# Stores from GpSimd's queue, and the recurrence stage's instruction order planned with other durations and with transfer queues that work in order

## The chip, the cores and the metric

The kernel runs on one core of one Trainium2 chip. The metric is the time of one execution on the device, in microseconds (us), as the median of several runs. In what follows PE is TensorE, DVE is VectorE, ACT is ScalarE, POOL is GpSimd and SP is SyncE. The engines work in parallel. Each takes its own instructions in the order in which the program holds them, and waits on semaphores for what the others make. SP computes nothing here: it issues DMA transfers.

## The reference, cut to what matters

Two requests, x_prompt and x_sample (512 tokens of 1024 features each, float32), pass through the same two layers. Layer 0 is a bidirectional RWKV-7 time mixing with 16 heads of 64, layer 1 a two-dimensional neighbourhood attention.

```python
def _wkv7_scan(r, decay, k, v, a, b, reverse):
    def step(s, inp):
        r_t, w_t, k_t, v_t, a_t, b_t = inp
        sa = jnp.einsum('bhvk,bhk->bhv', s, a_t)
        s = s * w_t[:, :, None, :] + sa[..., None] * b_t[:, :, None, :] + v_t[..., None] * k_t[:, :, None, :]
        return s, jnp.einsum('bhvk,bhk->bhv', s, r_t)
...
    # _rwkv7_branch: r, k, v are products of shifted inputs, z of the input
    kk = kk / jnp.maximum(jnp.sqrt(jnp.sum(kk * kk, axis=-1, keepdims=True)), 1e-12)
    for d in range(2):
        w_log = -jax.nn.softplus(-(w0[d] + jnp.tanh(xw @ w1[d]) @ w2[d]).astype(f32)) - 0.5
        decay = heads(jnp.exp(-jnp.exp(w_log)))
        a = heads(jax.nn.sigmoid((a0[d] + (xa @ a1[d]) @ a2[d]).astype(f32)))
        k_d = k * (1.0 + (a - 1.0) * k_a_h)
        ys.append(_wkv7_scan(r, decay, k_d, v, -kk, kk * a, reverse=(d == 1)))
...
def _trunk(x, ...):
    for i in range(DEPTH):
        xn = _rms_norm(x, pre_norm_g[i])
        h = _rwkv7_branch(xn, ...) if i % 2 == 0 else _natten_branch(xn, ...)
        x = x + _rms_norm(h, post_norm_g[i])
```

## The kernel before

Activations lie with features on the 128 partitions and the 512 tokens along the free dimension, so a request is 8 tiles of 128x512. A large product of a 128-column block of a weight with a request is built from 8 *triples*: weight and input are each split into a high and a low fp32r part, and a triple is three 128x512 matmuls (lines 404 to 406 outside the recurrence stage, 738 to 740 inside it). The split of a weight costs one ACT cast and one DVE subtraction per half (lines 699 and 701).

The program has three stages. The **prelude** normalises both requests and computes z and k of the first. The **recurrence stage** (`scan_phase`) computes both requests' time mixing. The **rest** does the attention layer.

In the recurrence stage each request has 4 head groups, so there are 8 groups in a row. The scan runs in chunks of 64 tokens, 8 *steps* per group, 64 steps in all, each needing the state S of the step before. Beside this chain of steps run these threads:

- `flow` (line 699 and on): the large products that the stage still owes, 76 columns of 8 triples, 608 triples in all, always in the same order: r and v of request 0, k, r and v of request 1, the output product of request 0, z of request 1, and then the first products of the attention layer. They fill PE while the chain of steps waits.
- `prep`: for each group, the factors `ab` of both scan directions, stored to DRAM as `dab` (1024 KB each store), and the Gram blocks (line 886).
- `inverse`: for each group, the inverse of a triangular matrix by 30 elimination rounds on DVE (lines 928, 929) and small matmuls (957, 959); its result MT is also cleared in part by POOL (line 946).
- `fetch`, `fetch_x`: loads of `cab`, `V` and `X` of each step from DRAM (`dab`, `dvt`).
- `near`, `outer`: the parts of a step that need no state (lines 1005, 1009 and 1030, 1038, 1045).
- `step`: lines 1075 and 1081 make Z, ACT copies it (1087), 1097 applies MT, ACT copies X (1108), 1113 and 1118 make the new state and the output, DVE scales the state (1123).
- `finish`: normalises the output of a group, multiplies by z and stores y.

Some gates tie the chain to the flow: a group's steps begin when its columns of v exist (`fetch` in `scan_phase`). The fifth group is the first of request 1 and needs 34 columns, 272 triples, of the flow. The seventh group waits until the fifth is finished, which needs z of request 1: 50 columns, 400 triples.

The order in which PE, DVE and ACT get the instructions of this stage is decided when the program is built. `weave` asks which thread could go on now, and the class `Clock` is its planner: it keeps a model time for every engine, adds a duration to it for every instruction recorded (`one`, `matmul`), and tells when a tile will be ready (`at`) or a buffer free (`room`). The lowest rank among the threads that are ready comes next. For SP the model only adds 380 ns per transfer; it does not hold SP back when a transfer must wait for its data. The order on SP and POOL, and everything outside the stage, is set by the framework's scheduler.

All transfers, loads and stores alike, are issued by SP (`load` and `save`, lines 306 and 309, and two direct calls at 1389 and 1455). POOL does memsets only: 32 of them clear the pad column of the tile `e1` (line 828), one for each direction of each head pair.

## Time and profile before

| | us |
|---|---|
| median of 3 runs (1751.27 to 1755.62) | 1752.39 |
| profiled execution: span from first to last instruction | 1748.0 |
| PE busy in it | 1604.4 (92%) |
| DVE busy | 1213.3 (69%) |
| ACT busy | 973.6 (56%) |
| POOL busy | 24.1 (1%) |

The profiled execution has no time of its own beside its span, so the span is compared with the median: 4.4 us lie between them. The 16 DMA engines moved 336.26 MB. An engine's busy time is the union of its instructions' intervals. A matmul's interval holds its whole way through the array, and the next one starts before it ends; so two 64x64 matmuls of 222 ns each may follow each other much closer than 222 ns. Waits are put down to the event that came last. An `SPq` row is SP's queue: the time in which SP issues a transfer or waits to do so; it is not part of any busy time.

### The profile page before, as it was taken

To read this page: it belongs to the slowest core of one execution; us is meant where nothing else is said; L and a number is where in the kernel's file an instruction comes from. 1 tells how busy PE (TensorE), PEld (TensorE's weight loads), DVE (VectorE), ACT (ScalarE), POOL (GpSimd) and SP (SyncE) were. 2 spreads that over 40 slices of the span, in tenths; PEclk is the share of its full clock that TensorE was granted. 3 is DMA by queue.
4 is the path that set the end of the run, shared out by engine and by line. 5 is a ranking of instruction groups with operands and counts; after the bars stand their busy time and mean duration, and the time that the engine had idled before them with its cause. 6 is when DMAs were issued, how large, how long until landed. Compare 5 with 4: busy or idle time off the path is not lost.

```text
span 1748.0 us, 46203 instructions
## 1 busy us (share of the span) xinstructions
PE 1604.4 (92%) x18816; PEld 1228.1 (70%) x18816; DVE 1213.3 (69%) x2645; ACT 973.6 (56%) x1964; POOL 24.1 (1%) x94
## 2 busy tenths in 40 slices
PE   7999788998999996898998988999999999999998
PEld 6766665765766674666766676787777788777776
DVE  8976588788888569796888857423556686555564
ACT  5444665666664565666666444333556664555462
POOL 0000000000000000000000000000000000000000
PEclk9989988999999997999999989999999999999999
DMA  5436677685666657777556766554555347545552
GB/s 201 163 115 211 219 266 221 204 269 190 213 198 209 198 172 254 221 213 251 186 187 216 247 200 201 186 204 139 175 184 166 103 132 262 174 155 158 162 175 97
DMA packets 240821, 336.26 MB, mean 192 GB/s; under 512 B 53697, under 2 KB 119361, under 8 KB 240609
## 3 DMA queue, kind: packets, MB, share of 16 engines
q1 hardware_dynamic: 240608, 333.31, 58.7%
q8 instruction: 148, 2.42, 0.6%
q14 instruction: 65, 0.52, 0.1%
HBM read 227.71 MB, written 105.51 MB: 191 GB/s over the span
## 4 chain that ended last, share of the span: by engine, by line
PE 61%; DVE 17%; DMA 8%; ACT 7%; issue 5%; SPq 1%; DVEq 0%; ACTq 0%
PE pg L404 6%; PE pg L405 6%; PE pg L406 6%; PE pm L738 5%; PE pm L739 5%; PE pm L740 5%; PE pm L1331 3%; DVE etmp L928 2%; PE po L1359 2%; PE pt L1346 2%; DVE N L929 2%; PE pf L1030 2%; DVE ab L851 2%; DMA cab<-dab 2%; PE zy L404 1%
## 5 line engine op out<-in xcount | busy, mean ns | idle before, releaser
L738 PE MATMUL pm<-act,whi 128*128 128x512 f32 x608 | 268.6, 442 | 17.9 <-ACT whi L699 8.0
L739 PE MATMUL pm<-act,whi 128*128 128x512 f32 x608 | 246.8, 406 | 19.0 <-DVE act L723 18.7
L740 PE MATMUL pm<-act,wlo 128*128 128x512 f32 x608 | 245.1, 403 | 2.3 <-DVE wlo L701 2.3
L404 PE MATMUL pg<-act,whi 128*128 128x512 f32 x448 | 181.6, 407 | 0.4 <-ACT whi L353 0.4
L405 PE MATMUL pg<-act,whi 128*128 128x512 f32 x448 | 178.4, 398 | 0.0
L406 PE MATMUL pg<-act,wlo 128*128 128x512 f32 x448 | 177.9, 397 | 0.0
L354 DVE TENSOR_TENSOR wlo<-raw,whi 128x512 fp32r<-128x512 f32 x156 | 107.0, 688 | 93.3 <-ACT whi L353 80.5
L353 ACT CAST whi<-raw 128x512 fp32r<-128x512 f32 x156 | 96.2, 618 | 131.6 <-PE pg L405 62.5
L701 DVE TENSOR_TENSOR wlo<-raw,whi 128x512 fp32r<-128x512 f32 x152 | 103.2, 686 | 84.4 <-ACT whi L699 83.1
L738 PEld LDWEIGHTS pm<-act,whi 128*128 128x128 f32 x608 | 117.7, 194 | 54.9 <-ACT whi L699 9.3
L739 PEld LDWEIGHTS pm<-act,whi 128*128 128x128 f32 x608 | 118.3, 195 | 44.9 <-DVE act L723 24.3
L740 PEld LDWEIGHTS pm<-act,wlo 128*128 128x128 f32 x608 | 118.3, 195 | 30.2 <-DVE wlo L701 4.4
L699 ACT CAST whi<-raw 128x512 fp32r<-128x512 f32 x152 | 93.0, 618 | 73.0 <-PE pm L739 55.8
L404 PEld LDWEIGHTS pg<-act,whi 128*128 128x128 f32 x448 | 84.3, 188 | 24.5 <-issue 9.1
L405 PEld LDWEIGHTS pg<-act,whi 128*128 128x128 f32 x448 | 84.3, 188 | 18.4 <-issue 3.5
L406 PEld LDWEIGHTS pg<-act,wlo 128*128 128x128 f32 x448 | 84.2, 188 | 18.2 <-issue 2.2
L929 DVE TENSOR_TENSOR N<-etmp,N 128x30 f32<-128x30 f32 (+14 forms) x240 | 79.8, 332 | 8.2
L1342 ACT ACTIVATE sb<-sb,mx 128x256 f32<-128x256 f32 x128 | 64.1, 502 | 37.6 <-DVE mx L1341 37.1
L928 DVE TENSOR_TENSOR etmp<-N 128x30 f32<-128x30 f32 (+14 forms) x240 | 78.7, 328 | 4.4
L1339 DVE CUSTOM_DVE_ANT_0 sb<-pm,bias 128x256 f32<-128x256 f32 x128 | 50.3, 421 | 45.1 <-PE pm L1331 34.2
L1045 ACT COPY Tm<-pf 128x512 f32<-128x512 f32 x56 | 32.8, 586 | 86.5 <-DVE R L1038 86.5
L1030 PE MATMUL pf<-cab 64*64 64x128 f32 (+1 forms) x2048 | 71.8, 279 | 9.3 <-DMA cab<-dab 6.8
(369 smaller groups left out, 3372.1 us busy)
## 6 DMA issues: line engine op xcount, KB each, us to landing
dab<-ab SPq DMA_DIRECT2D x32, 1024.0 KB, 5.8
cab<-dab SPq DMA_DIRECT2D x64, 512.0 KB, 4.5
raw<-in_w_in_dram SPq DMA_DIRECT2D x128, 256.0 KB, 3.0
bias<-in_rpb_dram SPq DMA_DIRECT2D x32, 384.0 KB, 4.3
raw<-in_w_z_dram SPq DMA_DIRECT2D x32, 256.0 KB, 4.4
dz<-tmp SPq DMA_DIRECT2D x32, 256.0 KB, 2.3
raw<-in_w_k_dram SPq DMA_DIRECT2D x32, 256.0 KB, 3.2
dk<-tmp SPq DMA_DIRECT2D x32, 256.0 KB, 2.2
```

The lines of the kernel that those rows point to most:

```text
L353: self.nc.scalar.copy(hi, src)
L354: (eng or self.nc.vector).tensor_tensor(lo, src, hi.bitcast(F32), op=ALU.subtract)
L404: nc.tensor.matmul(ps, hi, x[k][0], start=(k == 0), stop=False)
L405: nc.tensor.matmul(ps, hi, x[k][1], start=False, stop=False)
L406: nc.tensor.matmul(ps, lo, x[k][0], start=False, stop=(k == KT - 1))
L701: nc.vector.tensor_tensor(lo, raw.pop(h), hi.bitcast(F32), op=ALU.subtract)
L738: nc.tensor.matmul(ps, hi[:, at], xh, start=(k == 0), stop=False)
L739: nc.tensor.matmul(ps, hi[:, at], xl, start=False, stop=False)
L740: nc.tensor.matmul(ps, lo[:, at], xh, start=False, stop=(k == KT - 1))
L928: vt.tensor_tensor(tv, N[:, q + 1:, q:q + 1].broadcast_to([P, n, q]), N[:, q:q + 1, :q].broadcast_to([P, n, q]), op=ALU.mult)
L929: vt.tensor_tensor(N[:, q + 1:, :q], tv, N[:, q + 1:, :q], op=ALU.add)
L1030: end = nc.tensor.matmul(f[half(a), h, 0, d, g] if st.last else f[half(a), h, :, d, g], ab[half(h), d, g, 2 * e[d] + a], rt if st.last els ...
```

## The change

Three things are changed.

**Stores.** A new method `store` issues a transfer from POOL's queue. `save`, the stores of `dss`, `drn`, `dvt` and `dab`, and both stores of the outputs go through it. Of the 1290 transfers 358 move from SP to POOL. Loads stay on SP. A load of what a store wrote still waits for that store.

**The planner.** `Clock` gets other durations and latencies, a cost for ACT's function tables, and a queue `Q` for POOL's transfers (1000 ns each). SP and `Q` now work in order in the model: a transfer that must wait for its data or its buffer holds the ones behind it. Three gates on loads ask whether the buffer is free before the thread is chosen. The threads, their ranks and their gates are the same otherwise. The computation is the same.

**The pad of e1.** One tile `e1` with a pad column at either end takes the place of one per direction; it is cleared once, ahead of the stage.

```diff
-    LAT = dict(P=200.0, A=45.0, D=45.0, G=90.0, S=0.0)
+    LAT = dict(P=200.0, A=125.0, D=118.0, G=150.0, S=0.0, Q=0.0)
...
+    def free(self, tag, pool, bufs):
+        x = self.room((tag, id(pool)), bufs)
+        return x if x < 1e11 else 0.0
...
+            if e == "G" and "DMA" in type(i).__name__.upper():
+                e = "Q"
...
-                    if f != e or e == "S":
+                    if f != e or (e in "SQ" and table is self.made) or (table is self.made and e != "P"):
                         t = max(t, at)
...
-        elif e == "S":
-            self.t[e] = issued = max(issued, self.t["P"]) + 380.0
+        elif e in "SQ":
+            issued = self.t[e] = max(t, self.t["P"]) + (380.0 if e == "S" else 1000.0)
+            if e == "Q":
+                self.t["G"] = issued
...
-                c = 175.0 + 0.86 * n
...
+            if table != self.table:
+                c += 1283.0
+            return c + (50.0 if bank(ins[0]) else 90.0) + (2.0 if wide else 0.835) * n
...
     def save(self, kind, s, p, src):
         self.sp[kind, s, p] = d = self.dram(f"{kind}{s}{p}", src.shape)
-        self.nc.sync.dma_start(d, src)
+        self.store(d, src)
+
+    def store(self, dst, src):
+        self.nc.gpsimd.dma_start(dst, src)
...
-            e1 = b("e1", (P, NCH, L + 1))
-            pad = L * d
-            gps.memset(e1[:, :, pad:pad + 1], 1.0)
-            e1v, e0v = e1[:, :, 1 - d:L + 1 - d], e1[:, :, d:L + d]
+            e1 = self.e1
+            e1v, e0v = e1[:, :, 1:L + 1], e1[:, :, 2 * d:L + 2 * d]
...
-            self.load(sp["ab", s, pb][:, :, d, g, :].rearrange("c p a -> p c a"), ab.rearrange("p c a t -> p c (a t)"))
+            self.store(sp["ab", s, pb][:, :, d, g, :].rearrange("c p a -> p c a"), ab.rearrange("p c a t -> p c (a t)"))
...
-                        nc.sync.dma_start(self.a["y"][1][ms, j * T:j * T + T], hs[j, m])
+                        self.store(self.a["y"][1][ms, j * T:j * T + T], hs[j, m])
...
                 yield (
                     "S", lambda: did["states"] >= q - 1 and did["preps"] > st.n and ("v", st.s, 2 * st.pb + 1) in self.made,
-                    lambda c: c.at([self.sp["ab", st.s, st.pb].tensor.name]))
+                    lambda c: max(
+                        c.at([self.sp["ab", st.s, st.pb].tensor.name]), c.free("V", self.front, self.NX),
+                        max(c.used.get(self.cab[q % 2].tensor.name, {}).values(), default=0.0)))
```

The instructions of PE and DVE are the same in number and kind before and after. On ACT there are 6 more loads of a function table, 30 for 24. What moves is the order. Three places show how.

The first is PE between the last step of the second group and the first of the third. Before, from one L1097 (the application of MT) to the next, these are the first 12 rows of 19; `pm` with `act` and `whi` or `wlo` is a flow triple, the rest belongs to steps, `prep` and `inverse`:

```order
L1097 MATMUL us_6177<-Z_6148,MT_440_1697 64x64 x8
L1005 MATMUL zy_6118<-cab_441_1698 64x64 x8
L959 MATMUL pm_6198<-MT_439_1696,NA_5837 32x32 x32
L1118 MATMUL zy_6118<-X_5959,R_6015 64x64 x8
L625 MATMUL pm_6250<-tmp_6238,cc 2x512
L1081 MATMUL zy_6268<-V_5990,AK_6188 64x64 x8
L1030 MATMUL pf_6280<-cab_442_1699 64x2x64 x16
L807 MATMUL pm_6303<-h_127_637,w2h_5917 128x512
L808 MATMUL pm_6303<-h_127_637,w2l_5916 128x512
L959 MATMUL pm_6309<-MT_439_1696,NA_5837 32x32 x32
L807 MATMUL pm_6351<-h_138_673,w2h_5917 128x512
L808 MATMUL pm_6351<-h_138_673,w2l_5916 128x512
```

With the change the same place begins like this (lines are those of the changed kernel: 1122 is the old 1097, 1143 the old 1118, 765 to 767 the old 738 to 740):

```order
L1122 MATMUL us_5798<-Z_5780,MT_441_1700 64x64 x8
L765 MATMUL pm_5482<-act_4054,whi_4960 128x512
L766 MATMUL pm_5482<-act_4053,whi_4960 128x512
L767 MATMUL pm_5482<-act_4054,wlo_4961 128x512
L1143 MATMUL zy_5748<-X_5608,R_5699 64x64 x8
L765 MATMUL pm_5482<-act_4307,whi_4960 128x512
L766 MATMUL pm_5482<-act_4306,whi_4960 128x512
L767 MATMUL pm_5482<-act_4307,wlo_4961 128x512
L765 MATMUL pm_5858<-act_2518,whi_5166 128x512
L766 MATMUL pm_5858<-act_2517,whi_5166 128x512
L767 MATMUL pm_5858<-act_2518,wlo_5167 128x512
L765 MATMUL pm_5858<-act_3313,whi_5166 128x512
```

Before, 2 triples stand between these two steps; now 54 do. Over the stage, the triples that stand ahead of the first L1097 of the eight groups are 116, 159, 178, 210, 306, 334, 438 and 448 before, and 124, 159, 228, 255, 321, 397, 448 and 484 now. Ahead of the last L1097 of the fourth group stand 228 and now 275, of the sixth 354 and now 415; ahead of the last L1118 of all, 465 and now 508.

The second place is SP at the load of `k` for the second head pair of the sixth group. Before (`k`, `r`, `lora` are what `prep` loads, `raw` are weights for the flow; `dvt`, `dab`, `dks` and `dv` on the left are stores):

```order
L309 DMA dvt_1696_9187<-vs_9298 64x8x64 x2
L309 DMA dvt_1696_9187<-vs_9313 64x8x64 x2
L309 DMA dab_1661_9064<-ab_9273 128x8x256
L309 DMA raw_9337<-in_w_v_dram 128x512
L309 DMA k_9463<-dk_1080_5127 128x512
L309 DMA dvt_1696_9187<-vs_9403 64x8x64 x2
L309 DMA raw_9428<-in_w_v_dram 128x512
L309 DMA tmp_9471<-in_lora_dram 128x512
L306 DMA dks_1729_9401<-kp_1691_9173 128x512
L309 DMA r_9464<-dr_1553_8533 128x512
L306 DMA dv_1738_9438<-tmp_9436 128x512
L309 DMA dvt_1696_9187<-vs_9444 64x8x64 x2
```

With the change, SP at the same load (L336 is the new line of `load`):

```order
L336 DMA rb_9902<-drn_1266_6330 64x512 x2
L336 DMA bv_12051<-dv_1570_8438 128x512
L336 DMA raw_9633<-in_w_o_dram 128x512
L336 DMA raw_9694<-in_w_o_dram 128x512
L336 DMA k_9900<-dk_1038_4965 128x512
L336 DMA xr_9876<-dy_1241_6204 128x512
L336 DMA tmp_9908<-in_lora_dram 128x512
L336 DMA r_9901<-dr_1322_6646 128x512
L336 DMA xr_9995<-dy_1563_8425 128x512
L336 DMA raw_9868<-in_w_o_dram 128x512
```

Of the 12 rows before, 7 are stores; none of the rows is one now.

The third place is POOL at the inverse of the first group. With the change:

```order
L333 DMA dvt_628_2470<-vs_2963 64x8x64 x2
L333 DMA dvt_628_2470<-vs_2973 64x8x64 x2
L333 DMA dab_647_2533<-ab_2829 128x8x256
L971 MEMSET MT_440_1699 32x32x32 x2
L333 DMA dks_743_3085<-kp_691_2722 128x512
L333 DMA dv_745_3089<-tmp_3087 128x512
```

Before, this memset of MT (the old L946) had only pads of `e1` around it on POOL:

```order
L828 MEMSET e_660_2580 128x8
L828 MEMSET e_686_2727 128x8
L828 MEMSET e_758_3104 128x8
L946 MEMSET MT_439_1696 32x32x32 x2
L828 MEMSET e_784_3291 128x8
L828 MEMSET e_874_3858 128x8
```

The memset now stands behind stores, each of which holds POOL's queue until its data are made.

More of the change, by code (lines that the diff above doesn't have):

```diff
@@ L67, in __init__ @@
         self.seen = 0
+        self.table = "exp"
     def skip(self):
@@ L160, in one, with cost @@
                 u[e] = max(u.get(e, 0.0), done)
-        return 0.0 if e == "S" and "dram" in str(type(outs[0].bass_ap.tensor)).lower() else done
+        return 0.0 if e in "SQ" and disk(outs[0]) else done
+    def cost(self, e, i, ins, outs, n, free, name):
+        kind = type(i).__name__
+        bank = lambda x: name(x).startswith(self.BANKS)
+        per = 105.0 if e == "A" else 58.0
+        c = per * sum(free(x) == 1 and n > 1 and not bank(x) for x in ins[1:])
+        if e == "A":
+            func = str(getattr(i, "func", "")).split(".")[-1]
+            table = "root" if func == "Sqrt" else "exp" if func in ("Exp", "Tanh") else self.table
+            if table != self.table:
+                c += 1283.0
+            self.table = table
+            wide = outs[0].ap[-1][0] > 8 or ins[0].ap[-1][0] > 8
+            return c + (50.0 if bank(ins[0]) else 90.0) + (2.0 if wide else 0.835) * n
+        if e == "G":
+            return c + 150.0 + n
+        c += 66.0
+        if "Reciprocal" in kind:
+            return c + 6.2 * n
+        if getattr(i, "is_tensor_tensor_scan", False):
+            return c + 2.09 * n
+        if "Transpose" in kind:
+            return c + 1.8 * n
+        one = len([x for x in ins if free(x) > 1]) <= 1 and "TensorTensor" not in kind and "Reduce" not in kind
+        if one and not any(bank(x) for x in ins + outs):
+            return c + 0.52 * n
+        return c + 1.045 * n
     def matmul(self, i, ins, n, t):
@@ L166, in matmul @@
         if not f32:
-            c = 0.4375 * n + 3
+            c = 0.4535 * n + 3
         elif tr:
@@ L630, in column @@
                 sp["ss", s] = self.dram(f"ss{s}", (16, T))
-            self.load(sp["ss", s][2 * p:2 * p + 2], row)
+            self.store(sp["ss", s][2 * p:2 * p + 2], row)
             self.made.add((kind, s, p))
@@ L643, in column @@
                 sp["rn", s, 0] = self.dram(f"rn{s}", (16, T))
-                self.load(sp["rn", s, 0].rearrange("a (b c) -> (a b) c", b=8), rn)
+                self.store(sp["rn", s, 0].rearrange("a (b c) -> (a b) c", b=8), rn)
                 self.made.add(("rn", s))
@@ L663, in column @@
             for j in range(2):
-                self.load(
+                self.store(
                     sp["vt", s][p // 2, j, :, :, :, d, p % 2].rearrange("m h t c -> t (m h) c"),
@@ L690, in loads @@
                 for j in range(2):
-                    yield "S", lambda: did["load"] < did["split"] + self.NRAW
+                    yield "S", lambda: did["load"] < did["split"] + self.NRAW, lambda c: c.free("raw", self.main, self.NRAW)
                     raw[2 * c + j] = self.load(self.t("raw", (P, self.WP), self.NRAW), src[:, j * self.WP:(j + 1) * self.WP])
@@ L832, in prep @@
             act.activation(e2, cw, AF.Exp, scale=CDEC)
-            act.copy(wc[:, d, g] if d == 0 else wc[:, d, g, ::-1], e1[:, :, L - pad])
+            act.copy(wc[:, d, g] if d == 0 else wc[:, d, g, ::-1], e1[:, :, 1 if d else L])
             ck = max(self.clock.room(("ab", id(self.pp)), 1), 0.0)
@@ L1388, in out1 @@
             (nc.vector if k % 2 else nc.vector).tensor_tensor(h, h, x, op=ALU.add)
-            nc.sync.dma_start(self.a["y"][s][k * P:(k + 1) * P, :], h)
+            self.store(self.a["y"][s][k * P:(k + 1) * P, :], h)
             yield
@@ L1517, in scan_phase @@
             self.nc.vector.tensor_copy(self.mrx[:, d], self.mr[d].unsqueeze(1).broadcast_to([P, 2, L]))
+        self.e1 = self.t("e1", (P, NCH, L + 2), 1, F32, self.pp)
+        for pad in (0, L + 1):
+            self.nc.gpsimd.memset(self.e1[:, :, pad:pad + 1], 1.0)
         self.MTb = [t(f"MT{j}", (P, 32, 2, 32)) for j in range(2)]
@@ L1547, in fetch_x @@
                 st = self.steps[q]
-                yield "S", lambda: did["steps"] >= q - 1 and did["fetch"] > q
+                yield "S", lambda: did["steps"] >= q - 1 and did["fetch"] > q, lambda c: c.free("X", self.front, self.NX)
                 self.fetch_x(st)
```

29 lines of the change are left out of this document (9 added, 20 removed).

## The prediction

> **What bounds the kernel now.** I read the page first, then the busy times of the engines by stage, then who waited for whom within the recurrence stage, then the chain of waits and SP's own timeline where the chain runs through transfers.
>
> ```profile
> span 1748.0 us, 46203 instructions
> ...
> PE 1604.4 (92%) x18816; PEld 1228.1 (70%) x18816; DVE 1213.3 (69%) x2645; ACT 973.6 (56%) x1964; POOL 24.1 (1%) x94
> ...
> PE 61%; DVE 17%; DMA 8%; ACT 7%; issue 5%; SPq 1%; DVEq 0%; ACTq 0%
> ```
>
> The 92% is a mean over stages with different limits. The windows by stage (columns: window, its length, busy time and instructions of PE, PEld, DVE, ACT, POOL, granted clock, DMA share, GB/s) separate them:
>
> ```profile
> 0.00:175.00 175.00, 157.04 (x636) 118.06 (x636) 143.67 (x268) 83.26 (x141) 1.86 (x44) 0.96 0.49 172
> 175.00:633.00 458.00, 404.80 (x7524) 302.67 (x7526) 351.40 (x667) 285.04 (x575) 13.22 (x29) 0.96 0.69 218
> 633.00:749.00 116.00, 93.47 (x1093) 70.01 (x1090) 92.97 (x164) 75.50 (x145) 2.57 (x8) 0.87 0.69 220
> 749.00:1106.00 357.00, 316.11 (x6269) 245.36 (x6264) 272.16 (x530) 199.18 (x391) 6.48 (x13) 0.96 0.65 209
> 1106.00:1192.00 86.00, 86.00 (x392) 70.08 (x392) 33.11 (x48) 33.34 (x55) 0.00 (x0) 1.00 0.57 196
> 1192.00:1741.00 549.00, 546.95 (x2919) 421.95 (x2918) 317.26 (x965) 296.23 (x657) 0.00 (x0) 1.00 0.49 160
> ```
>
> From 175 to 1106 the chain of steps runs; there PE is idle for 931 − (404.80 + 93.47 + 316.11) = 116.6 us. From 1106 to 1192 the flow's triples that are left over run alone: 86 us without a gap, 392 matmuls, 0.219 us each. After 1192 PE is idle for 2 us in 549, so no transfer and no order of ACT or DVE can gain anything there. The stage is where the change can act. When the chain of steps ends is in the rows of its last matmul line:
>
> ```profile
> L1118 PE MATMUL zy<-X,R x1024: 221/222/369, 328.0 to 1107.5; 128*64 128x64 f32 x171
> ```
>
> And it is not even: windows of L1097 alone show two long holes, before the fifth group and before the seventh (the 15 are the tail of the sixth):
>
> ```profile
> 633.50:748.00 114.50, 0.00 (x0) 0.00 (x0) 0.87 0.69 219
> ...
> 893.50:985.00 91.50, 0.59 (x15) 0.41 (x11) 0.94 0.61 204
> ```
>
> The waits of the stage (engine, waiting line, what ended the wait: us, times, longest) name many short causes for PE and one pattern for SP:
>
> ```profile
> PE pm L739 <- DVE act L723: 18.7, 8, 4.9
> PE us L1113 <- ACT X L1108: 9.3, 15, 1.7
> PE us L1097 <- ACT Z L1087: 8.6, 11, 2.0
> ...
> PE pf L1030 <- DMA cab<-dab: 6.8, 5, 3.5
> ```
>
> ```profile
> SPq L306 <- ACT tmp L612: 31.0, 16, 6.7
> SPq L306 <- ACT tmp L1201: 25.1, 6, 6.7
> ...
> SPq L309 <- DVE ab L851: 16.2, 14, 2.7
> ...
> SPq L306 <- DVE tmp L1241: 11.9, 6, 5.4
> ```
>
> These SP rows are stores that wait for what they store; every load behind them waits too. Added, they are 31.0 + 25.1 + 16.2 + 11.9 = 84.2 us.
>
> **The stores, part by part.** On the chain of waits, transfers of 1 us or more stand 26 times between 175 and 1106, 109 us in all, 12% of the stage. The first and the last, and the first and last of the seven among them that are stores:
>
> ```profile
> 175.89 2.78 DMA xr<-dlv
> ...
> 266.83 4.78 DMA dab<-ab
> ...
> 703.19 6.27 DMA k<-dk
> ...
> 1027.18 4.03 DMA dy<-bv
> ...
> 1079.35 4.20 DMA X<-dvt
> ```
>
> SP's timeline around that load of k shows how it comes about:
>
> ```profile
> 699.03 2.68 SPq L309 DMA_DIRECT2D dvt<-vs  x4
> 701.81 0.65 SPq L309 DMA_DIRECT2D dab<-ab  x1
> 702.56 0.58 SPq L309 DMA_DIRECT2D raw<-in_w_v_dram  x1
> 703.19 1.27 SPq L309 DMA_DIRECT2D k<-dk  x1
> 704.56 2.02 SPq L309 DMA_DIRECT2D dvt<-vs  x2
> ```
>
> SP issues without a pause, and from 699.03 to 703.1 five of its six transfers are stores (2.68 + 0.65 of 4.1 us). With the change they are gone from this queue; the order of SP shows no store at this place. What that gives: SPq is 1% of the chain, 17 us, and 358 of 1290 transfers leave SP, 28%, so 5 us. Of the 84.2 us in which stores held SP, I count what stands on the chain at the chain's own share of transfers, 12%: 10 us. Together −15 us. The bounds: 0, if the loads are hidden anyway, and −40 us, if the loads on the chain (26 less 7 stores, some 80 us) come in half the time.
>
> [...]
>
> What the stores lose: nothing in this trace issues a transfer from POOL. The nearest rows are SP's issue of an output store and POOL's own memset of MT:
>
> ```profile
> L1455 SPq DMA_DIRECT2D out_dram<-oa x8: 332/338/401, 1733.2 to 1744.9; - x8
> ...
> L946 POOL MEMSET MT<- x16: 942/945/951, 297.0 to 1013.1; 32x1024 f32 x16
> ```
>
> I take POOL's 0.945 us for an issue, 0.6 more than SP's 0.338, since it is the one duration of that engine at work on a tile. It costs 7 x 0.6 = 4 us for the seven stores on the chain, and 1 us at the end, where the last two output stores follow one another; +5. The bounds are 0 and, if each were as long as SP's 2.02 us row above, 7 x 2.02 = +14. In the prelude and after 1192 the stores' move counts nothing: PE is covered there by 549 us of matmuls with 2 us idle, and in the prelude DVE, busy 143.67 of 175 us, stands in front of the stores; if POOL is late in giving back the four buffers of `ls`, some 5 us could come on top.
>
> **The pad of e1.** 32 memsets go. POOL is busy 24.1 us in the whole span, no wait of another engine on them is among the rows, so 0.
>
> **The order.** The kinds and numbers of PE's and DVE's instructions stay; ACT has six more table loads:
>
> ```profile
> L1161 ACT ACT_TABLE_LOAD x5 | 6.4, 1283 | 0.1
> ```
>
> 6 x 1.283 = 7.7 us on ACT, which is busy 559.7 of the stage's 931 us (60%). About half will meet an idle ACT: +4 us, bounds 0 and +8.
>
> The gain is in the triples. Ahead of the last L1118 stand 508 of 608 instead of 465: 43 triples, 129 matmuls, go from the stretch after 1106, where each costs 0.219 us of full time, into the stage, where PE has 116.6 us idle. 129 x 0.219 = 28 us; it fits four times. If the last step comes no later than now, −28 us. Why it should not come later: the hole before the fifth group is one that the gates make. This group needs 272 triples of the flow; ahead of the fourth group's last step stand 228 now and 275 with the change. The seventh needs 400; 354 stand ahead of the sixth's end now, 415 with the change. So 44 and 46 triples, 90 x 3 x 0.219 = 59 us at the best pace, no longer have to pass between two groups. Against it, 50 more triples stand before the third group (54 between two steps where there were 2): 33 us at that pace. Before the sixth group 62 stand as well. The balance, 59 − 33, is what I leave for the sixth group and count at 0. It is covered by the holes' 206 us; if they stay as they are, the third group's 33 us are lost (first rival).
>
> The waits of PE for DVE and ACT (18.7, 9.3, 8.6 us and shorter ones) may also shrink, as the planner now gives ACT and DVE some 120 ns until a result is seen, where it had 45. I count 0, since the steps are not fuller: between L1081 and L1097 fewer than 0.7 us of PE's work stand in 36 of 64 steps, 27 before (counted in the two orders at the paces of the trace). The bound is half of the idle that is left, (116.6 − 28) / 2 = 44 us.
>
> **The sum**: −28 (triples) −15 (loads) +5 (stores) +4 (tables) = −34 us. The span is 1748.0 us and the median of the runs 1752.39, so 4.4 us lie around the span; I take the same for the changed kernel: a span of about 1714 and a time of 1718 us. A measurement of this kernel can tell about 0.3% (5 us) from no change.
>
> **The rivals.**
>
> *The late third group (slower).* The 50 triples before it move every later group back by 33 us, and the holes before the fifth and the seventh, whose other causes (`prep`, `inverse`) remain, do not shrink. Then the last step is 33 us later, 28 are won after it, the loads lie beside longer waits and win nothing, and the 9 us of stores and tables stay: 1752 + 33 − 28 + 9 = 1766 us. For it: in the first hole PE is idle 22.5 of 116 us at a clock of 0.87, so flow alone does not make the hole. Against it: the missing triples do account for 44 and 46 of what runs in the holes. It decides if the two holes together shrink by less than some 20 us. Chance 0.18.
>
> *POOL's queue as the bound.* A store holds POOL until its data are made, and the memset of MT, on which the first step of a group depends, stands behind a `dab` store. If that costs 3 us in each of 8 groups and the seven stores on the chain wait for as much as DVE's longest instruction,
>
> ```profile
> L936 DVE STREAM_TRANSPOSE NA<-N 128x1024 f32<-128x1024 f32 x8 | 17.2, 2150 | 0.1
> ```
>
> it is 24 + 7 x 2.15 = 39 us against the 34: 1757 us, at the edge of no change. [...] Chance 0.10, half of it slower.
>
> *The triples delay the steps one for one.* Each stands in PE's queue ahead of a step, the last step comes 28 us later and the first term is 0: 1746 us, slightly faster. Chance 0.10, four tenths of it within 0.3%.
>
> *The order works as planned.* Half the remaining idle goes, −44 more, and loads at −25: some 1665 to 1695. Chance 0.15.
>
> **How the numbers follow.** My forecast has 0.47, with a range of its own from 1700 to 1738. Faster by over 0.3%: 0.47 + 0.15 + 0.06 = 0.68. Within 0.3%: 0.04 and 0.05 of the two middle rivals, 0.09. Slower: 0.18 + 0.05 = 0.23. The range goes from 1675, inside the last rival, to 1770, beyond the first.
>
> **What would show it.** The third group begins here now:
>
> ```profile
> 496.09 0.75 PE L1097 MATMUL us<-Z,MT 64*64 64x64 f32 x15
> ```
>
> Right: the last L1118 before 1107 in a span of about 1714; the stretch without steps after it near 58 us; the hole before the fifth group under 90 us; no wait of SP for ACT's tmp rows; PE idle in the stage under 90 us. Wrong: the third group's first L1097 over 30 us later than 496 us with holes as before; waits for `dab`, `dvt` or MT with POOL ahead of them; loads on the chain no shorter than before.

## The result, and the profile after

The changed kernel takes 1780.61 us, the median of 4 runs (1776.02 to 1783.8), beside 1751.83 us for the kernel before: a ratio of 1.015 on record, with a 95% interval from 1.0128 to 1.0172. The two medians differ by 28.8 us, where 34 us of gain were forecast, and the time is outside the range (1675 to 1770). The ratio is the number to compare with the experiments, which are ratios too; 1.015 is 26 us.

A profile is one execution. The undisturbed executions of the kernel before that the runs list, some 80, span 1742.8 to 1760.7 us, and the profiled one, 1748.0, is 5 us below their median; so a difference of some 5 us between two profiles can be chance. Time and span lie 1.7 to 2.1 us apart in every run, not 4.4 us as the prediction took it: the rest was this one execution.

From the page of the changed kernel, the same three lines as before:

```profile
span 1780.6 us, 46355 instructions
...
PE 1631.2 (92%) x18816; PEld 1240.9 (70%) x18816; DVE 1209.6 (68%) x2645; ACT 981.6 (55%) x1970; POOL 236.9 (13%) x422
...
PE 44%; issue 22%; DVE 8%; ACT 5%; POOL 2%; DMA 2%; POOLq 0%; SPq 0%; ACTq 0%; DVEq 0%
```

PE runs the same 18816 matmuls but is busy 26.8 us longer. That is the first thing to explain: no matmul was added. The chain is of little use here: a fifth of it is "issue", time for which the profile shows no releaser, so what follows rests on windows and waits. The last matmul line of a step in the changed kernel, from the view of that line:

```profile
L1143 PE MATMUL zy<-X,R x1024: 222/222/366, 327.9 to 1158.5; 128*64 128x64 f32 x171
```

The steps end at 1158.5, not before 1107: 51 us later. The windows by stage (columns as in the prediction) are cut where the steps end and where the flow's last triple ends, first of the kernel before, then of the changed one:

```profile
175.00:1107.80 932.80, 816.17 (x14892) 619.28 (x14892) 716.53 (x1360) 561.28 (x1112) 22.28 (x50) 0.95 0.67 214
1107.80:1208.10 100.30, 100.30 (x442) 82.18 (x443) 37.26 (x54) 37.06 (x61) 0.00 (x0) 1.00 0.56 191
1208.10:1748.00 539.90, 530.85 (x2848) 408.62 (x2847) 315.79 (x964) 291.96 (x651) 0.00 (x0) 1.00 0.49 161
```

```profile
175.00:1158.50 983.50, 865.83 (x15014) 653.27 (x15014) 721.11 (x1373) 575.54 (x1131) 157.25 (x235) 0.92 0.65 209
1158.50:1229.80 71.30, 71.30 (x323) 58.30 (x319) 28.68 (x42) 27.47 (x46) 7.58 (x14) 1.00 0.61 205
1229.80:1780.60 550.80, 536.03 (x2848) 410.15 (x2846) 317.03 (x964) 293.30 (x651) 37.53 (x69) 0.99 0.49 158
```

Three things stand in them. The stretch after the steps fell from 100.3 to 71.3 us, 29 us, which is the 28 us that the prediction worked out (its own cut, at 1192, ended that stretch early). The steps' part grew by 50.7 us. And the part after the flow, where the prediction counted nothing, grew by 10.9 us. The granted clock in the steps' part fell from 0.95 to 0.92, which is where the longer busy time of PE comes from.

The holes between groups in the changed kernel, before its third, fifth, sixth and seventh group:

```profile
480.00:564.00 84.00, 70.98 (x773) 48.73 (x772) 70.22 (x134) 53.57 (x97) 12.43 (x20) 0.84 0.57 188
693.50:775.40 81.90, 64.71 (x783) 49.43 (x782) 59.34 (x117) 46.20 (x86) 26.14 (x38) 0.85 0.73 218
828.00:909.30 81.30, 73.42 (x834) 55.31 (x824) 73.41 (x141) 60.40 (x107) 12.04 (x18) 0.84 0.65 218
968.00:1018.00 50.00, 42.48 (x570) 32.33 (x569) 43.76 (x74) 31.10 (x55) 7.64 (x12) 0.92 0.64 211
```

The holes before the fifth and the seventh shrank from 114.5 and 91.5 us to 82 and 50, as forecast (the fifth's below 90). But the third group begins at 564.26, 68 us later than 496.09, and there is a new hole of 81 us before the sixth (and one of 35 before the eighth).

SP no longer waits for a store's data. Its longest waits are, as before, for the buffers of its loads, and they grew (the first row was 201.6 us). Its waits for the landing of a store that a load reads back grew too; the largest row of them, for `dy`, was 22.3 us:

```profile
SPq L336 <- DVE wlo L381: 312.5, 119, 20.0
...
SPq L336 <- DMA dy<-bv: 44.3, 14, 5.4
```

What POOL pays for the stores (busy us, then mean ns of one issue):

```profile
L333 POOL DMA_DIRECT2D dvt<-vs x64 | 44.3, 698 | 91.8 <-ACT vs L689 86.4 <-issue 3.1 <-ACT Z L1112 2.2
L333 POOL DMA_DIRECT2D dab<-ab x32 | 29.0, 905 | 136.7 <-DVE ab L876 111.4 <-issue 14.9 <-DVE acc L1238 5.9
```

An issue takes 0.70 and 0.91 us in these two, the costliest kinds, and about 0.55 in the others, no more than the 0.945 that was assumed. The issue alone is not the loss.

### The profile page after: what moved, and what is told of

It reads as the page before. It is cut to its first block, busy times and chain, and to the rows that moved or that the text cites. A ratio compares the mean times of both kernels' runs of the same rounds, so it can differ in the third digit from the quotient of the medians.

```text
span 1780.6 us, 46355 instructions
## 1 busy us (share of the span) xinstructions
PE 1631.2 (92%) x18816; PEld 1240.9 (70%) x18816; DVE 1209.6 (68%) x2645; ACT 981.6 (55%) x1970; POOL 236.9 (13%) x422
## 3 DMA queue, kind: packets, MB, share of 16 engines
q1 hardware_dynamic: 138304, 227.77, 40.6%
## 4 chain that ended last, share of the span: by engine, by line
PE 44%; issue 22%; DVE 8%; ACT 5%; POOL 2%; DMA 2%; POOLq 0%; SPq 0%; ACTq 0%; DVEq 0%
PE pm L765 5%; PE pg L431 4%; PE pg L432 4%; PE pg L433 4%; PE pm L766 4%; PE pm L767 4%; PE pm L1356 2%; PE pf L1055 1%; PE po L1384 1%; PE zy L1143 1%; DVE etmp L953 1%; PE pt L1371 1%; PE us L1122 1%; PE us L1138 1%; DVE N L954 1%
## 5 line engine op out<-in xcount | busy, mean ns | idle before, releaser
L765 PE MATMUL pm<-act,whi 128*128 128x512 f32 x608 | 272.7, 449 | 15.2 <-ACT act L748 9.6
L766 PE MATMUL pm<-act,whi 128*128 128x512 f32 x608 | 249.4, 410 | 12.7 <-DVE act L750 12.0
L765 PEld LDWEIGHTS pm<-act,whi 128*128 128x128 f32 x608 | 119.2, 196 | 61.0 <-ACT act L748 13.7
L766 PEld LDWEIGHTS pm<-act,whi 128*128 128x128 f32 x608 | 120.6, 198 | 38.7 <-DVE act L750 17.4
```

Of the source, the lines that this page charges most:

```text
L765: nc.tensor.matmul(ps, hi[:, at], xh, start=(k == 0), stop=False)
L766: nc.tensor.matmul(ps, hi[:, at], xl, start=False, stop=False)
```

## The experiments

Two theories at first. **A**: the new order costs the time, since `prep` and `inverse` come late for the third and the sixth group. **B**: the stores cost it, since on POOL each lands later. Under A there were two sub-theories, A1 (the planner's queues in order) and A2 (its durations). In all kernels that are called "in its own order" the order of PE, DVE and ACT in the recurrence stage is that of the kernel named. The order of SP's loads is not held: where stores leave SP, the framework orders its queue anew. With all stores on POOL some 80 of the 932 loads stand at another place than in the kernel before, and no run separates this from the move itself.

### The change taken apart

*The stores alone*, in the order of before:

```diff
+            if e == "G" and "DMA" in type(i).__name__.upper():
+                e = "S"
...
-        self.nc.sync.dma_start(d, src)
+        self.store(d, src)
+
+    def store(self, dst, src):
+        self.nc.gpsimd.dma_start(dst, src)
...
```

> The kernel before with its 358 stores issued by POOL; the planner books them as it booked SP's, so the order of PE, DVE and ACT in the recurrence stage stays that of before. Theory A (the new order costs the time): the stores are worth between -15 and +5 us, a ratio of 0.991 to 1.003 and a third group that begins within 5 us of 496. Theory B (the stores cost it, since on POOL each lands about 1 us later than on SP): 1.010 to 1.017, the third group at 520 or later.

Measured: 1.0148 (1.01 to 1.0197), the third group at 503.4.

*The order alone*, with the stores on SP:

```diff
-            if e == "G" and "DMA" in type(i).__name__.upper():
+            if e == "S" and len(i.outs) and hasattr(i.outs[0], "bass_ap") and i.outs[0].bass_ap.tensor.name.startswith("d"):
                 e = "Q"
...
-        self.nc.gpsimd.dma_start(dst, src)
+        self.nc.sync.dma_start(dst, src)
```

> The changed kernel with its stores issued by SP again; the planner books them as it books POOL's, so the order in the recurrence stage stays that of the changed kernel. Theory A: 1.012 to 1.025 of the time before, the third group's first L1122 at 550 or later. Theory B: 0.99 to 1.003, the third group below 520.

Measured: 1.0017 (0.9998 to 1.0036), the third group at 557. So theory A falls for this kernel: the third group is 61 us late by the order alone, and the loss that goes with it is at most 0.4%. Theory B's two ratios hold. Its two statements on the third group do not: it is at 503 where B said 520 or later, and at 557 where B said below 520. Where the third group begins says nothing of the time here. *The pads alone*, `e1` as one tile:

> The kernel before with the one tile of e1 and its two pad columns set once, all else and the order as before. All theories: 0.998 to 1.002. Rival (one e1 tile makes the second direction's Exp wait for the readers of the first's): 1.003 to 1.01, waits of ACT's e for DVE's ab.

Measured: 1.0 (0.9982 to 1.0018). The parts add up: 1.48% for the stores (26 us), 0.17% for the order (3 us) and nothing for the pads make 1.65%, against 1.5% (1.28 to 1.72).

### Which stores, and how they cost

With the order of DVE and PE the same, instruction by instruction, the kernel before and the one with stores on POOL can be laid side by side. The lag of DVE grows in jumps. The first large one: SP's store of `ab` and DVE's next write of `ab` in the kernel before,

```profile
231.15 0.37 SPq L309 DMA_DIRECT2D dab<-ab  x1
```

```profile
236.41 0.69 DVE L851 TENSOR_TENSOR ab<-r,e 128x512 f32<-128x512 f32 x1 [0.24 <-ACT wc L835]
```

and the same place with the stores on POOL, where the first row is DVE's last write of `ab` ahead of the store, followed by PE:

```profile
233.10 0.69 DVE L856 TENSOR_TENSOR ab<-kp,u 128x512 f32<-128x512 f32 x1
...
242.59 0.69 DVE L856 TENSOR_TENSOR ab<-r,e 128x512 f32<-128x512 f32 x1 [3.75 <-DMA dab<-ab]
```

```profile
234.09 0.91 POOL L311 DMA_DIRECT2D dab<-ab  x1 [1.94 <-DVE ab L856]
```

```profile
245.14 0.77 PE L744 MATMUL pm<-act,whi 128*128 128x512 f32 x1 [3.48 <-DVE act L728]
245.71 0.63 PE L745 MATMUL pm<-act,wlo 128*128 128x512 f32 x1
...
249.22 0.40 PE L744 MATMUL pm<-act,whi 128*128 128x512 f32 x1
```

`ab` has one buffer. The last write of it ends at 233.79, POOL issues the store at 234.09, it lands at about 242.5, and until then DVE, which takes its instructions in order, stands still. The flow's `act` stands behind it on DVE, so PE stands still too, 3.48 us. Then PE runs its first matmuls of the flow at 0.6 us a piece instead of 0.4. In the changed kernel the same matmuls take 0.63 us where the granted clock is 0.50 and 0.39 where it is 1.00 (at 536 and 540 us). From the start of the issue to the landing (last number, median us) in the kernel before and with the stores on POOL:

```profile
dab<-ab SPq DMA_DIRECT2D x32, 1024.0 KB, 5.8
...
dz<-tmp SPq DMA_DIRECT2D x32, 256.0 KB, 2.3
dk<-tmp SPq DMA_DIRECT2D x32, 256.0 KB, 2.2
```

```profile
dab<-ab POOLq DMA_DIRECT2D x32, 1024.0 KB, 6.8
...
dz<-tmp POOLq DMA_DIRECT2D x32, 256.0 KB, 2.9
dk<-tmp POOLq DMA_DIRECT2D x32, 256.0 KB, 3.5
```

That is 0.6 to 1.3 us later each, of which 0.2 to 0.5 us are the longer issue. These medians are rough: in the kernel before the trace tells the landing of only 4 of the 32 stores of `dab`, 10 of `dz` and 9 of `dk`. For `dv` the same view has the opposite sign (5.6 us before, 3.7 on POOL), with 2 of 32 told. Theory D was formed from this (landing, and idle time that is paid again as half clock), with rival E (any transfer of POOL disturbs, by its number). Four kernels, all in the order of before. *Only ab's stores on POOL*, and *all but ab's*:

> The kernel before, in its own order, with only the 32 stores of ab on POOL; the other 326 stay on SP. Theory D (landing: a store of POOL is seen about 1 us later, what waits for it idles PE, and idle time costs again as half clock): ab has one buffer and its store is followed by loads of cab, so this part carries about half of the 26 us: a ratio of 1.005 to 1.010, with more waits of DVE's ab for the store and of PE for cab. Rival E (every transfer of POOL disturbs, by its number): 32 of 358 stores are a tenth, 1.000 to 1.003.

Measured: 1.0099 (1.0069 to 1.013).

> The kernel before, in its own order of the stage, with all stores on POOL but those of ab, which stay on SP. Theory D: the other half of the 26 us, of which some 10 after the stage: 1.005 to 1.011. Rival E: nine tenths of it, 1.011 to 1.015.

Measured: 1.0125 (1.0102 to 1.0148). The 32 stores of `ab`, a tenth of all, cost 17 us as D said, so E falls as the whole account. The second number lies in E's range and above D's: all stores but those of `ab` cost 22 us, of which the profile puts 11 into the stage and 12 behind the flow. So `ab` is not the only store that costs. The two halves make 39 us and not 26, so they are not additive; that a delay which stands behind another is paid only once would explain it, and is not shown. *A dose*: five memsets ahead of each store.

```diff
+    def store(self, dst, src):
+        for _ in range(5):
+            self.nc.gpsimd.memset(self.dly, 0.0)
+        self.nc.gpsimd.dma_start(dst, src)
```

> The kernel before, in its own order of the stage, with all stores on POOL and five memsets of 120 columns, about 1 us, ahead of each store on POOL. Theory D: the landing is late by twice as much, so the loss is about twice as large: 1.025 to 1.035. Rival E, or a loss at fixed places (the end of the program, the queue's start): as with the stores alone, 1.011 to 1.019.

Measured: 1.0527 (1.0493 to 1.0561), more than either theory said. DVE's waits for ab's store from 175 to 1210 us (us, times, longest) in the kernel before, with the stores on POOL, and with the dose:

```profile
DVE ab L851 <- DMA dab<-ab: 3.3, 2, 2.3
```

```profile
DVE ab L856 <- DMA dab<-ab: 13.5, 7, 3.7
```

```profile
DVE ab L859 <- DMA dab<-ab: 50.4, 10, 15.0
```

The dose was not the even 1 us that was meant. The memsets pile up ahead of a store where stores come close together, as POOL's timeline shows at the longest wait:

```profile
525.03 11.98 POOL L313 MEMSET dly<- 128x120 f32 x47
...
537.07 4.55 POOL L313 MEMSET dly<- 128x120 f32 x18
541.92 0.90 POOL L314 DMA_DIRECT2D dab<-ab  x1 [0.30 <-issue]
```

It confirms the place, and not the size per microsecond. The counter-test, a second buffer for `ab`, was not run.

In the changed kernel's own order the place is another. The same wait for `ab`, in the order alone and in the changed kernel:

```profile
DVE ab L876 <- DMA dab<-ab: 3.8, 3, 2.3
```

```profile
DVE ab L876 <- DMA dab<-ab: 4.4, 2, 2.5
```

The changed kernel's flow still ends 18 us later than with the order alone. Laid side by side in the same way, the largest jump of PE's lag, 5.4 us, comes at the first `prep`. With the stores on SP:

```profile
180.00 0.54 SPq L333 DMA_DIRECT2D drn<-tmp  x1
```

```profile
183.38 1.11 SPq L336 DMA_DIRECT2D rb<-drn  x2
184.54 0.58 SPq L336 DMA_DIRECT2D k<-dk  x1
```

```profile
191.47 0.51 PE L835 MATMUL pm<-h,w2l 128*128 128x512 f32 x1 [1.69 <-DVE w2l L820]
```

and in the changed kernel:

```profile
182.50 0.54 POOL L333 DMA_DIRECT2D drn<-tmp  x1 [0.52 <-DVE tmp L669]
```

```profile
179.14 8.54 SPq L336 DMA_DIRECT2D raw<-in_w_r_dram  x5
188.78 1.16 SPq L336 DMA_DIRECT2D rb<-drn  x2
190.04 0.52 SPq L336 DMA_DIRECT2D k<-dk  x1
```

```profile
196.24 0.79 PE L835 MATMUL pm<-h,w2l 128*128 128x512 f32 x1 [7.06 <-DVE w2l L820]
```

The load `rb` reads back what `drn` stores. It goes out 3.4 us after the issue of that store with the stores on SP, and 6.3 us after it with the store on POOL. SP holds the load of `k` behind it, DVE waits 7.2 us for `k` where it waited 1.1, and PE stands behind DVE. Two things overlap here. SP's new order puts five loads of weights right ahead of `rb`, where the order alone has two, and their issue ends at 187.7; then SP waits 1.0 us more for `drn` to land. So D and the new order of SP's loads can't be told apart at this place. Two smaller jumps, 1.4 and 1.3 us where PE is at 771 and 774 us, come behind ACT's waits for the buffer of `vs`, whose store has not landed (2.9 and 2.1 us; 1.0 and 0.5 with the order alone). Those are waits for a landing, as D has it, at `dvt`. The rest of the 18 us lies in jumps of 2 us and less that were not taken apart.

*Relief of SP without POOL*: ACT issues the stores of what it has made.

```diff
-        self.save(kind, s, p, o)
+        self.sp[kind, s, p] = dd = self.dram(f"{kind}{s}{p}", o.shape)
+        act.dma_start(dd, o)
...
```

> The kernel before, in its own order, with the stores that ACT has made (r, k, v, the sums ss, vt) issued by ACT instead of SP: SP is relieved and POOL is not used. If SP's relief is worth what the prediction gave it: 0.990 to 0.997. If relief is worth nothing: 0.998 to 1.004, the stores landing as fast as from SP. If the issue holds ACT up: 1.005 and more.

Measured: 1.0158 (1.0133 to 1.0183). Its stores of `dvt` land in 2.7 us (3.4 from SP), but ACT's timeline shows what an issue holds up:

```profile
306.50 1.29 ACTq L667 DMA_DIRECT2D dvt<-vs  x2
307.84 0.63 ACT L799 ACTIVATE km<-rb 128x512 f32<-128x512 f32 x1 [1.36 <-issue]
```

That is about 0.64 us for each of the 64 stores of `vs`, some 41 us on the engine that the steps wait for. The ratio is the one forecast for an issue that holds ACT up; that these 41 us make it is not shown. Whether relief of SP is worth anything by itself is left open by this run.

*The outputs alone on POOL*, for the 10 us after the flow:

> The kernel before with only the stores of the two outputs on POOL; the order of the stage stays, that of PE after the stage shifts a little, since the framework orders it itself. Theory D with the tail: with all stores on POOL, the work after the flow's end took 550.2 us instead of 539.9, and from the last issue of a store to the end of the span 7.0 us instead of 2.8. That should come back here whole, since the last stores are outputs: +8 to +12 us, a ratio of 1.004 to 1.007, the stage unchanged within 5 us. Rival (the 10 us come from the stores of dq, dk, dv, dz and dxt after the flow's end): 0.999 to 1.003, with the last issue some 7 us ahead of the end all the same.

Measured: 1.0023 (1.0 to 1.0045). After the flow it takes 543.6 us, 3.7 more; the kernel with only the pads changed, where nothing differs there, took 544.5, so one profile can't tell that from nothing. (Over all kernels with the outputs' stores on SP this part takes 539 to 545 us, so of the 10 us that the stores on POOL add to it some 5 are clear of chance.) The last issue of a store ends 3.4 us before the end of the span. With all stores on POOL it is 7.0 us, from this row to 1782.4:

```profile
1774.20 1.20 POOL L311 DMA_DIRECT2D out_dram<-oa  x2 [2.92 <-DVE oa L1459]
```

and 2.8 us in the kernel before. So the rival's ratio holds, and not its 7 us at the end: 4 of the 10 us lie at the end of the program, and they go with the number of stores on POOL, not with the last ones alone. Why is not shown, and the other 6 are not settled.

### Half clock

The clock in windows of 2 us in the changed kernel's hole before its third group (first number after the length: PE busy; the third from the end: granted clock):

```profile
518.00:520.00 2.00, 0.49 (x3) 0.09 (x2) 1.90 (x5) 1.72 (x4) 0.54 (x1) 1.00 0.92 327
520.00:522.00 2.00, 1.39 (x4) 0.32 (x2) 2.00 (x5) 1.14 (x2) 0.28 (x1) 0.87 0.93 310
522.00:524.00 2.00, 2.00 (x66) 1.31 (x66) 1.93 (x6) 0.66 (x2) 0.24 (x1) 0.50 0.10 33
...
536.00:538.00 2.00, 2.00 (x6) 1.52 (x6) 1.90 (x7) 0.68 (x2) 0.54 (x1) 0.50 0.50 188
538.00:540.00 2.00, 2.00 (x9) 1.60 (x8) 1.90 (x7) 0.48 (x1) 0.00 (x0) 0.86 0.70 219
```

PE was idle for 1.5 us of the first window; the clock fell at about 521.5 (1.00 up to there and 0.50 behind it make the row's 0.87) and, with further waits in between, came back at about 538.5, 17 us later. Added over windows of 1 us (1 less the granted clock), this spell cost 8.54 us. From 175 to 1230 us the changed kernel has 19 such spells and the kernel before 17, and each of them cost 1.70 or 1.71 us or a multiple of it, up to seven times; at a clock of 0.50 that is 3.4 us and its multiples. PE was not idle for that long ahead of this spell: of the 3.4 us up to 521.5 it was idle for 1.7. What decides when the clock falls and when it comes back is not shown.

So the stage has a balance. From 175 us to the flow's end, idle time (length less PE's busy time), the loss to the half clock (an upper bound, since it counts idle time at half clock too), and the rest:

| kernel | ratio | length | idle | half clock | rest |
|---|---|---|---|---|---|
| before | 1 | 1033.1 | 116.6 | 51.0 | 865.5 |
| stores on POOL, old order | 1.0148 | 1057.2 | 125.9 | 66.3 | 865.0 |
| new order, stores on SP | 1.0017 | 1036.4 | 108.3 | 59.5 | 868.6 |
| the changed kernel | 1.015 | 1054.8 | 117.7 | 74.8 | 862.3 |
| all but ab on POOL | 1.0125 | 1044.4 | 124.7 | 49.3 | 870.4 |
| only ab on POOL | 1.0099 | 1055.0 | 131.8 | 56.2 | 867.0 |

The rest hardly moves in these six. The stores add 9 us of idle time and 15 us of half clock; the new order takes 8 us of idle time away and pays the same back in half clock. Two cautions. The kernels with only the pads or only the outputs' stores changed, which have the stage of before, show 120.8 and 119.5 us of idle time and 46.1 and 52.9 of half clock, so a term is good to about 5 us. And idle time does not always come back as half clock: with all stores but ab's on POOL 8 us more of it cost 11 us of stage, with ab's alone 15 cost 22, with the dose 61 cost 87, and with all stores 9 cost 24. That is 1.4 to 2.6 us of stage for 1 us of idle time.

### The order

Theory G: the stage is as long as this balance says, and which triple stands ahead of which step decides nothing. (The rest is what is left over, so the balance alone cannot prove it: over all the kernels of this document it goes from 844 to 878 us, and is low where the upper bound for the half clock is high.) The first pair, with the stores still on POOL:

> The changed kernel whose planner books transfers as before (a transfer's wait for its buffer or its data holds nothing behind it; 0.38 us an issue on each queue, the old times to land); new durations, gates, POOL stores and pads stay. Theory A1 (the booking in order holds the first steps of prep back, since every step that begins with a load waits until SP is free in the plan): the third group begins 30 us or more earlier than in the changed kernel's 564, the ratio is 1.00 or below. Theory A2 (the durations do it): 1.012 to 1.018 as now, the third group at 550 or later.

Measured: 1.0159 (1.0122 to 1.0197). The third group begins at 554. By these two numbers it is A2. The steps end 17 us earlier than in the changed kernel, the flow 9 us later.

> The changed kernel whose planner gives ACT, DVE and POOL the old 45, 45 and 90 ns until a result is seen; all else stays. Theory A2: 1.00 or below, the third group at 530 or earlier. Theory A1: 1.010 to 1.025, the third group at 550 or later.

Measured: 1.0555 (1.0527 to 1.0584), with 171.6 us idle and 110.6 of half clock, and the third group at 561. A2 said 1.00 or below, and A1 no more than 1.025, so neither holds: under the new costs the short old latencies make the order much worse. But the new latencies in the old planner are worth little:

```diff
-    LAT = dict(P=200.0, A=45.0, D=45.0, G=90.0, S=0.0)
+    LAT = dict(P=200.0, A=125.0, D=118.0, G=150.0, S=0.0)
```

> The kernel before with one line of the planner changed: the new 125, 118 and 150 ns until a result is seen, for 45, 45 and 90; costs, queues, stores as before. Theory G (any order leaves the stage as long as its work at full clock, some 865 us, plus PE's idle time and what the half clock takes; which triple stands ahead of which step decides nothing): 0.995 to 1.012, with the last step and the stretch after it moving against each other. Rival (the latencies are what the order needs; the prediction's order that works as planned): 0.975 to 0.993, idle PE in the stage under 100 us.

Measured: 0.9977 (0.9957 to 0.9997), as G said; idle time is 107.5 us. Then the new planner with the old booking of transfers and all stores on SP:

```diff
-            issued = self.t[e] = max(t, self.t["P"]) + (380.0 if e == "S" else 1000.0)
...
+            self.t[e] = issued = max(issued, self.t["P"]) + 380.0
...
-            done = self.dq + 800.0
...
+            done = max(self.dq, t + 800.0 + c) + 670.0
```

> The changed kernel with all stores on SP and the planner's transfers as before; new durations, gates and pads stay. With the stores on POOL the same order ended its steps 17 us ahead of the changed kernel's and the flow 9 us behind it. Theory G: within 0.5% of the kernel before and of the order with new queues, 0.997 to 1.007. Rival (the booking of queues in order is what is worth something, hidden under POOL's stores so far): 1.007 to 1.02.

Measured: 0.9959 (0.9934 to 0.9984), just below G's range (its interval reaches into it) and below the new order's 1.0017; the rival falls. To see whether that is more than a draw, both planners were disturbed by a few ns:

> The order of the changed kernel with all stores on SP (which took 1.0017 of the time before), replanned with ACT's and DVE's latency in the planner 5 and 3 ns lower (120, 115). Theory J (the plan is a draw: a change of a few ns moves the time by as much as the choice of the queue model): somewhere between 0.990 and 1.012, more than 0.3% from 1.0017. Rival K (the booking of queues in order is what costs, 0.6%): 0.999 to 1.005, as the order was.

> The same with 130 and 121 ns. Theory J: another draw between 0.990 and 1.012, at least one of this pair more than 0.3% from 1.0017. Rival K: 0.999 to 1.005.

> The order planned with the old transfers and all stores on SP (0.9959), replanned with 120 and 115 ns. Theory J: between 0.988 and 1.010, the two pairs overlap. Rival K: 0.993 to 0.999, both of this pair below both of the other.

> The same with 130 and 121 ns. Theory J: between 0.988 and 1.010. Rival K: 0.993 to 0.999.

And without the new gates (`c.free` and the one on `cab`), two plans:

> The changed kernel with all stores on SP, the planner's transfers as before and the four new gates (raw, V, X, cab) taken out: of the change the new durations, latencies and pads are left. If the booking in order is what costs (its three plans gave 1.0017, 1.0189, 1.036; the three with the old transfers 0.9948, 0.9959, 1.0007) and the gates are nothing without it: 0.992 to 1.002. If the gates are worth something by themselves: 1.002 to 1.015.

> The same with 120 and 115 ns in place of 125 and 118: a second plan, so that one draw does not decide. The same numbers: 0.992 to 1.002, or 1.002 to 1.015 if the gates are worth something.

Measured, all with stores on SP (in brackets the interval; then the first matmul of the sixteenth prep, the end of the steps, and the balance's two terms):

| transfers in the planner | ratio | last prep | steps end | idle | half clock |
|---|---|---|---|---|---|
| before | 1 | 905 | 1107.8 | 116.6 | 51.0 |
| in order, 125 ns | 1.0017 (0.9998 to 1.0036) | 972 | 1140.4 | 108.3 | 59.5 |
| in order, 120 ns | 1.036 (1.0311 to 1.0408) | 995 | 1174.3 | 143.1 | 105.0 |
| in order, 130 ns | 1.0189 (1.0155 to 1.0222) | 949 | 1130.7 | 130.5 | 81.7 |
| as before, 125 ns | 0.9959 (0.9934 to 0.9984) | 920 | 1112.7 | 111.9 | 54.4 |
| as before, 120 ns | 0.9948 (0.9927 to 0.9969) | 923 | 1109.9 | 107.7 | 47.6 |
| as before, 130 ns | 1.0007 (0.9985 to 1.003) | 927 | 1119.4 | 110.6 | 54.4 |
| as before, no gates, 125 ns | 0.9952 (0.9935 to 0.9969) | 909 | 1110.9 | 104.6 | 40.8 |
| as before, no gates, 120 ns | 0.9985 (0.9964 to 1.0006) | 909 | 1105.2 | 109.7 | 45.9 |

The two new plans with queues in order, 1.036 and 1.0189, lie above both theories' ranges; of the two without, both lie in J's and one in K's. The three plans with queues in order lie all above the five without, which speaks for K's sign: the booking costs something. With so few plans that is no proof; the nearest two, 1.0017 and 1.0007, cannot be told apart, and were there no difference, three out of eight would come out on top once in 56 times. And 5 and 3 ns in two constants move one plan by 3.4%, more than J expected, so the order in the changed kernel was a lucky draw of its kind. The longest and the shortest stage of the table, as windows: first the queues in order at 120 ns, then the transfers as before without the gates at 125 ns (the durations only):

```profile
175.00:1277.30 1102.30, 959.24 (x15341) 729.40 (x15341) 754.73 (x1414) 602.91 (x1174) 18.67 (x18) 0.90 0.63 199
```

```profile
175.00:1198.20 1023.20, 918.61 (x15333) 698.88 (x15334) 745.98 (x1412) 602.25 (x1176) 18.73 (x18) 0.96 0.68 214
```

The first has as many matmuls, but for a few that the trace misses, 40.6 us more busy time and 38.5 us more idle time. In every plan with queues in order the last `prep` comes 22 us or more later than in any without. Why the booking delays it is only argued: in the planner a prep begins with loads, and a step waits until its queue is free in the plan. Without the gates both plans lie in the range for gates that are worth nothing (0.992 to 1.002).

With the stores on SP, the plans at 0.9948 (1744.44 us) and 0.9952 (1744.18 us, the durations only) are faster than both kernels, by half a per cent; with one plan each, that is a pick from draws.

## Why the prediction was wrong, point by point

**The stores (−15 and +5).** Here the sign was lost: −10 us were counted and +26 measured (17 to 34 by the interval). The issue was not undersized (about 0.55 to 0.91 us, 0.945 assumed). The step that failed is "what the stores lose", which priced only the issue, and only for seven stores on the chain. It left out the landing, 0.6 to 1.3 us later for `dab`, `dz` and `dk`, though `dab<-ab` stood on the chain with 4.78 us, and it left out who waits for a landing. In the old order that is above all DVE, for the one buffer of `ab` (13.5 us of waits, 3.3 before); in the changed kernel that wait is 4.4 us, and the largest single loss found, 5.4 us of PE, comes where SP's queue holds the load of `k` behind the one that reads `drn` back, in a new order of its loads. How the rest of the 26 us divides is open. The bound of +14 was made of issues too, and its row of 2.02 us holds two issues, so 1.01 us each. The gain on the other side is not seen: from issue to landing k takes 3.2 us as before, `cab` 4.7 instead of 4.5. (The chain that it was taken from holds 28 transfers and 118 us, where the prediction counted 26 and 109; that changes the 10 us by less than one.) No run isolates the relief of SP, so that it is worth nothing is not shown.

**PE's time as a constant.** All terms were made at 0.219 us a triple's matmul and with idle time as free room. It isn't: a matmul of the flow takes 0.6 us at half clock for 0.4, and the 9 us of idle time that the stores added stand beside 24 us of longer stage.

**The triples (−28).** The count was right (−29 after the steps). "If the last step comes no later" was the condition, and it came 33 us later with the stores on SP, 51 with them on POOL. The step that failed is "It fits four times": idle time that lies in waits of a few hundred ns to 3 us was not room for 28 us more of work: with the order alone it fell by 8 us, to 108.3, and the half clock took as much. What happened to the order alone is the third rival, the delay one for one: −29 and +33.

**The late third group.** This rival named what is seen, 68 us late, and gave 1766 us, nearest of all to the result. That is luck: its mechanism is not what decides. By the order alone the group is 61 us late at 1.0017, and in the changed kernel both old holes shrank by 74 us together, where its condition was less than 20.

**POOL's queue as the bound.** The right part of the change, at the wrong place: the memset of MT behind a store delays no one; the view of its line names no instruction that waited for it. The 7 x 2.15 us of this rival no run shows either: DVE is busy 1213.3 us before and 1214.3 with the stores alone on POOL, and in the changed kernel `dab` lands after 6.7 us in the median both where DVE is busy for under 60% of the 1.5 us behind the issue (7 stores) and where it is busy for 80% or more (18). Why a store lands later from POOL is open.

**The tail.** "Counts nothing" was off by 10 us, 4 of them after the last issue.

**The pads (0)** were right. **The waits of PE (0)**: its waits for ACT's Z were 8.6 us and are 9.8, and its idle time up to the flow's end is 117.7 us, not under 90, so nothing came of the bound of −44. **The six table loads (+4)** have no run of their own.

## What to carry over

Before a store is moved to another queue, look for the buffer that it frees and the load that reads it back: what counts is the time from the last write to the landing, and who stands in order behind the engine or the queue that waits for it. Where PE's clock falls with its idle time, price a new wait at more than its length (1.4 to 2.6 times in this stage), and don't book idle time as room. And where a planner's order moves by per cents when its constants move by a few ns, one plan says little about the model behind it: disturb it, and compare sets of plans.

## What was not expected of the hardware

- A store from POOL takes about 0.55 us to issue (0.70 for `dvt`, 0.91 for `dab`), beside 0.34 for an output store from SP. Stores of `dab`, `dz` and `dk` land 0.6 to 1.3 us later than from SP, by rough medians. ACT pays about 0.64 us for an issue of `dvt`.
- With 326 to 358 stores on POOL the program ends 5.6 to 9.1 us after the last issue; with 16 it is 3.4, with 32 (the last store being SP's) 3.0, with none 2.8.
- Behind a wait of PE of 1.5 us and 0.2 us more of idle time (518 to 521.5 us in the changed kernel) its granted clock fell from 1.00 to 0.50 and, with further waits of up to 2.5 us, stayed there for 17 us. The 19 spells of this kind in that stage, and the 17 in the kernel before, each cost 1.70 or 1.71 us or a multiple of it.
